# A hybrid decoder step on one core: token-row sums as a chain of their own, a new order for the first stage, and a shorter series for the decay

## The chip, the cores and the metric

The kernel runs on one core of a Trainium2 chip. The metric is device time in microseconds for one launch. Before the change three runs took 2071.05, 2072.48 and 2072.96 us; the median is 2072.48. One further execution was taken with the hardware profiler; it took 2066.42 us.

The engines are called as in the profile: PE (matmuls), PEld (its weight loads), DVE, ACT, POOL, and SP, which here only issues DMAs. An `ACTq` or `SPq` row is the issue of a DMA from that engine's queue.

## The reference

One layer of a hybrid decoder over 2048 prompt tokens and 8 decode tokens, width 1024:

```python
xn = _rmsnorm(x, norm1_g)
z = jnp.einsum('btd,de->bte', xn, w_in)
xr, gr, q, k, v = jnp.split(z, IN_SPLITS, axis=-1)
xc, new_conv = _causal_conv(xr, conv_buf, conv_w, conv_b)
hs, h_last = _rglru(xc, h0, ...)          # log_a = -8 * r * softplus(-lru_lambda)
rec = hs * jax.nn.gelu(gr)
att = _prompt_attention(q, k, v, sinks)   # sliding window 128, 8 heads, 2 kv heads, learned sinks
mix = concatenate([_rmsnorm(rec, rec_norm_g), _rmsnorm(att, attn_norm_g)])
h = x + jnp.einsum('bte,ed->btd', mix, w_out)
hn = _rmsnorm(h, norm2_g)
ff = jax.nn.silu(einsum(hn, w_gate)) * einsum(hn, w_up)
y = h + einsum(ff, w_down)                # then a final _rmsnorm; caches and states are returned too
```

The two places that the change edits in the computation are the mean of squares of each token's row, which `_rmsnorm(x, norm1_g)` needs, and `softplus(-lru_lambda)`, a value for each of the 512 channels of the recurrent branch. The rest of the change is order and time.

## The kernel before, in words

**Precision.** Every matmul is done as three: each operand is split into a rounded high part and the low rest, and `mm3` (matmuls at L388) adds high·high, high·low and low·high. A split of an activation costs one ACT pass (high, L417) and one DVE pass (low, L418); a split of a weight tile is a CAST on ACT (L360) and a subtraction on POOL (L361). Split weights of the input and output projections are stored to DRAM when first made (L380, `split_w`) and loaded back for later sub-blocks (L372).

**Stages.** The 2056 tokens are cut into four sub-blocks s = 0..3 (520 tokens, then three times 512). For each: `prep` loads the input transposed (`xs`, 8 tiles of 128 channels by 512 tokens) and splits it (`xn`); 14 units of the input projection (`ip{s}_{u}`) follow; then convolution, gates (`g`, ACT tanh into `ra` and `ia`) and scan for the recurrent branch; eight attention items per sub-block, each with scores `s`, exponentials into `sc`, transposes `pt` (copied to `pth` on ACT and `ptl` on DVE) and outputs `o` into `ratt`; two group norms (their sums are `st_rc`, `st_at`, their factors spread over partitions are `bc_rc`, `bc_at`); and the output projection `op`. After about 720 us only the feed-forward part (`ps_g`, `ps_u`, `pd`, `pw`) runs, in three token groups.

**Norm of the input.** The factor 1/rms of a token is not applied to `xn` but later, when the unit's PSUM is evicted: DVE multiplies by `rb_x`, the factors spread over all partitions (L743; outputs `xr`, `qraw`, `kraw`, `vraw`, `rrec`). For sub-block 0 the squares are summed over the transposed tiles. For sub-blocks 1 to 3 the tokens are also loaded as rows: `xt`, eight tiles of 128 tokens by 512 channels, 256 KB each, loaded by SP (L720) and squared on ACT with a running sum (L721). In `prep` one `xt` follows each `xs`; both take their buffers from the same pool `xsp`, which has two. After the eighth, `norm_rows` makes the factors: `xcols`, then `bc_x`, then `rb_x`.

**The decay's prologue.** `prologue` (from L607) computes softplus on DVE in tiles `sp` of 128 by 4 numbers with a series of ten terms: 1 + 8 x 2 + 1 instructions from L626 to L630. The convolution's gates of sub-block 0 need its result, `c` and `nc`.

**What sets the order.** Each of these functions is a generator that yields times. `Chains` runs them as events in order of these times, with keys such as ("xn", s) that one chain fires and another waits for. The time is the priority of the instructions, and a scheduler orders ACT, DVE, POOL and SP by it; `ahead(n)` gives an instruction a priority n earlier. The order of PE's matmuls is written out: `PE_ORDER` lists them by name with counts. Names with `w_` in front are fillers, matmuls on a matrix of ones whose result is overwritten. They go to the PSUM tile that the next matmul of that name uses. All engines and the DMA queues then run strictly in their own order, so an instruction that waits holds what stands behind it.

Of the kernel before, what the change touches and what calls it, by code (L numbers as in the profile page):

```python
# [13 lines left out]
P = 128  # L14
# [33 lines left out]
T_IP = [19.773, 89.475, 240.018, 361.589]  # L48
T_OP = [187.418, 329.004, 451.638, 498.253]
T_OPA, L_LM = 515.753, 37.593  # L50
# [75 lines left out]
ip1_0_0:6 dS:6 ip1_0_0:5 o3_0_0 ip1_0_0:4 ip1_12_0:2 dS2:2 ip1_12_0:2 pt3_0_1 o3_0_0 ip1_12_0:2 pt3_0_1:3
ip1_12_0:18 ip1_13_0:6 o3_0_1 ip1_13_0:2 o3_0_1 ip1_13_0:3 pt3_1_0:4 ip1_13_0:9 dS3 ip1_13_0 dS3 ip1_13_0:3
ip1_1_0:8 pt3_1_1:2 o3_1_0 pt3_1_1 ip1_1_0:2 pt3_1_1 o3_1_0 dS4:4 s4_0_0 ip1_1_0:2 dS4:4 o3_1_1 s4_0_1:4 s4_0_0:3
ip1_1_0 o3_1_1 ip1_1_0:11 ip1_5_0:6 dS5:2 s4_1_0:2 s4_1_1:4 ip1_5_0 vt1_1 ip1_5_0:3 s4_1_0:2 ip1_5_0:8 pt4_0_0:2
ip1_5_0 pt4_0_0:2 ip1_5_0:5 ip1_2_0:2 s5_0_0:4 ip1_2_0 s5_0_1:4 ip1_2_0 vt1_2 ip1_2_0:8 o4_0_0 ip1_2_0:6 pt4_0_1  # L130
o4_0_0 pt4_0_1:3 ip1_2_0:3 vt1_3 ip1_2_0:3 o4_0_1 s5_1_0:4 s5_1_1:4 o4_0_1 st_rc0 pt4_1_0:4 st_rc0:4 ip1_6_0:24
pt4_1_1:4 bc_rc0_0:3 s6_0_0:4 bc_rc0_0 s6_0_1:4 pt5_0_0 bc_rc0_4 pt5_0_0:3 g1_0_0_0 g1_0_1_0 w_st_at0:11 st_at0:5
ip1_3_0:24 ip1_7_0:8 bc_at0_0:4 ip1_7_0:16 op0_0_0:2 bc_at0_4 op0_0_0:10 op0_0_260:12 op0_1_0 g1_1_0_0 op0_1_0:11
op0_0_0 op0_0_260 op0_1_0 op0_0_260:2 op0_0_0:3 op0_1_0:6 op0_0_0:6 op0_1_0:3 op0_0_260:9 g1_1_1_0 op0_0_0:2
op0_1_0:2 o4_1_0:2 op0_1_260:4 o4_1_1:2 op0_1_260:20 op0_2_0:11 pt5_0_1:4 o5_0_0:2 op0_2_0:13 op0_2_260:13 s6_1_0:3
s6_1_1:4 s6_1_0 o5_0_1 op0_2_260:11 op0_3_0 g1_2_0_0 pt5_1_0 op0_3_0:12 o5_0_1 op0_3_0:2 pt5_1_0:3 op0_3_0:9
op0_3_260:17 g1_2_1_0 op0_3_260:7 op0_4_0:21 pt5_1_1:4 op0_4_0:3 op0_4_260:2 o5_1_0:2 op0_4_260:19 s7_0_0:4
op0_4_260:3 op0_5_0 o5_1_1 op0_5_0:12 pt6_0_0:4 op0_5_0 o5_1_1 op0_5_0:5 s7_0_1:4 op0_5_0:5 op0_5_260:7 g1_3_0_0
op0_5_260:17 o6_0_0 op0_6_0:3 pt6_0_1 o6_0_0 pt6_0_1:3 op0_6_0:5 g1_3_1_0 op0_6_0:10 o6_0_1 op0_6_0:6 op0_6_260
s7_1_0:4 s7_1_1:2 op0_6_260 s7_1_1:2 o6_0_1 op0_6_260 pt6_1_0:4 op0_6_260:21 op0_7_0:17 o6_1_0 bc_x2_0:3 pt6_1_1  # L140
o6_1_0 bc_x2_0 op0_7_0 pt6_1_1:3 op0_7_0:6 op0_7_260:5 o6_1_1 op0_7_260:19 ip2_4_0:24 o6_1_1 ip2_0_0:5 pt7_0_0:4
ip2_0_0:10 st_h0:5 ip2_0_0:2 o7_0_0 ip2_0_0:2 o7_0_0 ip2_0_0:5 ip2_5_0:4 pt7_0_1 st_rc1:2 pt7_0_1:3 st_rc1:2
ip2_5_0:9 pt7_1_0:4 ip2_5_0:2 o7_0_1 ip2_5_0:3 o7_0_1 bc_rc1_0:4 ip2_5_0:3 o7_1_0 ip2_5_0:3 pt7_1_1:3 ip2_1_0:2
pt7_1_1 ip2_1_0:8 g2_0_0_0 ip2_1_0:8 o7_1_0 ip2_1_0:4 o7_1_1 ip2_1_0:2 o7_1_1 g2_0_1_0 ip2_8_0:24 ip2_12_0:18
g2_1_0_0 ip2_12_0:6 ip2_9_0:23 g2_1_1_0 ip2_9_0 ip2_10_0:24 ip2_11_0:18 vt2_0 ip2_11_0:6 ip2_2_0:7 vt2_1 ip2_2_0:17
ip2_13_0:6 vt2_2 ip2_13_0:18 ip2_7_0:7 vt2_3 ip2_7_0:17 ip2_3_0:5 s8_0_0:4 s8_0_1:4 ip2_3_0:2 w_o8_0:2 st_at1:4
ip2_3_0:17 ip2_6_0 s8_1_0:4 s8_1_1 bc_at1_0:4 s8_1_1 pt8_0_0:3 s8_1_1 pt8_0_0 s8_1_1 ip2_6_0:7 s9_0_0:4 ip2_6_0:10
g2_2_0_0 ip2_6_0 o8_0_0 s9_0_1:4 ip2_6_0:5 op1_0_0:5 pt8_0_1 op1_0_0:2 o8_0_0 pt8_0_1:3 op1_0_0:4 g2_2_1_0
# [1556 lines left out]
```

## Time and profile before

| what | value |
|---|---|
| median of three runs | 2072.48 us |
| profiled execution | 2066.42 us, of which the span is 2064.6 us |
| PE busy | 2022.5 us, 98% |
| DVE, ACT, POOL busy | 1457.8, 945.4, 907.1 us |
| PE busy in 0 to 720 us | 693.80 us |
| PE busy in 720 to 2064 us | 1328.72 us |
| DMA | 450.98 MB, mean 218 GB/s |

The span is the time from the first to the last instruction in the trace. A row of the timeline tells start, length, engine, line, operation, output and inputs, and in brackets for how long the engine idled before and whose end released it. A row of a table by stage gives, for each engine, busy time and number of instructions, then the granted clock of PE (1.00 is full), the busy share of the 16 DMA engines and GB/s. Busy times of PE are modelled, since matmuls are pipelined. In a row like `L628 DVE TENSOR_TENSOR sp<-sp x8` the three numbers are the shortest, median and longest duration in ns, and the two times the first and last start.

### The profile page before, as it was taken

What the parts mean: (1) busy time and instruction counts of PE and PEld (TensorE: products, weight loads), DVE (VectorE), ACT (ScalarE), POOL (GpSimd) and SP (SyncE); (2) the same over time, 40 slices, a digit from 0 to 9 for tenths busy, and PEclk for the clock granted to TensorE, in tenths of its full rate; (3) what the DMA queues carried; (4) which work ended last, traced back from release to release, by engine and by line L of the source; (5) the groups of instructions that cost most, each with busy time, mean ns of one, the idle gap of its engine ahead of it and who ended that gap; (6) DMA issues with size and microseconds to landing.
All of it is one profiled execution on the core that took longest, in us unless ns stands there. A gap on an engine that the chain in (4) does not pass through costs nothing.

```text
span 2064.6 us, 34880 instructions
## 1 busy us (share of the span) xinstructions
PE 2022.5 (98%) x12328; PEld 1911.9 (93%) x12328; DVE 1457.8 (71%) x2702; ACT 945.4 (46%) x1960; POOL 907.1 (44%) x799
## 2 busy tenths in 40 slices
PE   8999899999999999999999999999999999999998
PEld 8988787878777899999999999999999999999998
DVE  7787785776996756666755667767767666777675
ACT  5764684563564543343334533334335433433343
POOL 5211343020122687657665655556556522322333
PEclk9999999999999999999999999999999999999999
DMA  8854485576687955655555777667677675566652
GB/s 302 272 203 149 153 299 168 183 258 195 205 267 261 329 201 203 219 209 207 199 190 191 251 255 245 232 228 229 211 255 265 215 246 193 187 195 195 197 179 96
DMA packets 208991, 450.98 MB, mean 218 GB/s; under 512 B 25232, under 2 KB 82720, under 8 KB 208800
## 3 DMA queue, kind: packets, MB, share of 16 engines
q1 hardware_dynamic: 205184, 445.73, 64.1%
q10 hardware_dynamic: 3632, 3.02, 0.4%
q8 instruction: 97, 1.59, 0.3%
q14 instruction: 78, 0.64, 0.1%
HBM read 335.89 MB, written 113.84 MB: 218 GB/s over the span
## 4 chain that ended last, share of the span: by engine, by line
PE 73%; DVE 11%; DMA 7%; ACT 4%; issue 3%; POOL 1%; SPq 0%; DVEq 0%; ACTq 0%; POOLq 0%
PE ps_u L388 18%; PE ps_g L388 18%; PE pd L388 11%; PE ip L388 10%; PE pw L388 9%; PE op L388 3%; DMA n<-hs 3%; DMA xt<-in_xR 1%; DMA mixed<-n 1%; PE o L388 1%; PE pt L393 1%; DVE sc L953 1%; PE s L388 1%; ACT sc L949 1%; DVE n L507 1%
## 5 line engine op out<-in xcount | busy, mean ns | idle before, releaser
L388 PE MATMUL ps_g<-hn,w_g 128*128 128x342 f32 (+1 forms) x2772 | 490.1, 320 | 3.2 <-DVE c_u L1386 1.8
L388 PE MATMUL ps_u<-hn,w_u 128*128 128x342 f32 (+1 forms) x2772 | 479.7, 319 | 0.5 <-ACT c_u L1412 0.4
L388 PEld LDWEIGHTS ps_g<-hn,w_g 128*128 128x128 f32 x2772 | 445.1, 188 | 5.2 <-DVE c_u L1386 2.7
L388 PEld LDWEIGHTS ps_u<-hn,w_u 128*128 128x128 f32 x2772 | 444.1, 188 | 1.1 <-ACT c_u L1412 0.7
L388 PE MATMUL ip<-xn,w_in 128*128 128x512 f32 (+1 forms) x1680 | 354.2, 358 | 4.5 <-DVE xr L743 2.0
L388 PEld LDWEIGHTS ip<-xn,w_in 128*128 128x128 f32 x1680 | 270.6, 189 | 50.4 <-issue 3.8
L1476 DVE TENSOR_TENSOR y<-y,pw 128x342 f32<-128x342 f32 x504 | 239.0, 504 | 75.1 <-PE pw L388 74.4
L388 PE MATMUL pd<-fh,w_d 128*128 128x344 f32 (+1 forms) x960 | 239.8, 320 | 0.0
L388 PE MATMUL op<-mix,w_out 128*128 128x512 f32 (+1 forms) x960 | 205.8, 360 | 0.1
L388 PEld LDWEIGHTS op<-mix,w_out 128*128 128x128 f32 x960 | 157.8, 192 | 28.7 <-issue 4.8
L1445 DVE TENSOR_TENSOR y<-y,pd 128x344 f32<-128x344 f32 (+1 forms) x240 | 117.9, 507 | 76.3 <-PE pd L388 71.5
L388 PEld LDWEIGHTS pd<-fh,w_d 128*128 128x128 f32 x960 | 168.3, 188 | 0.9 <-DVE y L1445 0.6
L388 PE MATMUL pw<-fh,wd 128*128 128x342 f32 x576 | 165.7, 320 | 2.1 <-DVE y L1476 2.1
L388 PE MATMUL pd<-fl,w_d 128*128 128x344 f32 (+1 forms) x480 | 153.5, 320 | 0.0
L1357 DVE TENSOR_TENSOR fl<-c_u,fh 128x342 fp32r<-128x342 f32 (+1 forms) x132 | 107.2, 817 | 45.5 <-ACT fh L1356 45.2
L1201 POOL TENSOR_TENSOR w_u<-ru,w_u 128x512 fp32r<-128x512 f32 x44 | 59.2, 1345 | 181.4 <-ACT w_u L1200 137.6
L1356 ACT CAST fh<-c_u 128x342 fp32r<-128x342 f32 (+1 forms) x132 | 63.1, 480 | 156.8 <-POOL c_u L1368 61.2
L1368 POOL TENSOR_TENSOR c_u<-c_u,c_g 128x342 f32<-128x342 f32 (+1 forms) x60 | 60.2, 1004 | 169.4 <-DVE c_u L1386 131.8
L388 PE MATMUL pw<-t,wd 128*128 128x342 f32 x648 | 126.8, 320 | 1.8 <-DVE t L1357 1.6
L1386 DVE TENSOR_TENSOR c_u<-c_u,ps_u 128x342 f32<-128x342 f32 (+1 forms) x99 | 50.3, 509 | 100.8 <-PE ps_u L388 100.5
L388 PEld LDWEIGHTS pw<-t,wd 128*128 128x128 f32 x648 | 106.0, 188 | 3.8 <-DVE t L1357 2.6
L388 PEld LDWEIGHTS pw<-fh,wd 128*128 128x128 f32 x576 | 105.3, 189 | 2.8 <-DVE y L1476 2.7
(313 smaller groups left out, 3509.7 us busy)
## 6 DMA issues: line engine op xcount, KB each, us to landing
w_g<-split_g SPq DMA_DIRECT2D x88, 512.0 KB, 4.2
w_u<-split_u SPq DMA_DIRECT2D x88, 512.0 KB, 4.6
w_in<-split_w SPq DMA_DIRECT2D x84, 512.0 KB, 3.6
rg<-in_wgate SPq DMA_DIRECT2D x110, 256.0 KB, 3.0
ru<-in_wup SPq DMA_DIRECT2D x110, 256.0 KB, 3.1
w_out<-split_w SPq DMA_DIRECT2D x48, 512.0 KB, 4.8
split_g<-w_g SPq DMA_DIRECT2D x44, 512.0 KB, 3.1
split_u<-w_u SPq DMA_DIRECT2D x44, 512.0 KB, 2.9
```

Of the source, the lines that this page charges most:

```text
L388: r = nc.tensor.matmul(*args, **kw)
L393: r = nc.tensor.transpose(*args)
L507: nc.vector.scalar_tensor_tensor(x, x, col(V_G2 + k), bc[n][:, :nn], ALU.mult, ALU.mult)
L949: nc.scalar.activation(sc[:, g, :kn + 1], sc[:, g, :kn + 1], AF.Exp, bias=mx[:, 0, g:g + 1], scale=-1.0, accum_out=mx[:, 1, g:g + 1])
L953: nc.vector.tensor_scalar(sc[:, g, :kn], sc[:, g, :kn], mx[:, 1, g:g + 1], None, ALU.mult)
L1201: lo_eng.tensor_tensor(w[:, 1, :], src, w[:, 0, :].bitcast(F32), op=ALU.subtract)
L1356: nc.scalar.copy(hi, v)
L1357: nc.vector.tensor_tensor(lo, v, hi.bitcast(F32), ALU.subtract)
L1368: (nc.vector if p == NPAIR - 1 or src is not v else eng(E_MUL[2 * h + n])).tensor_tensor(v, src, g, op=ALU.mult)
L1386: nc.vector.tensor_tensor(o, a, b, op)
L1445: r = nc.vector.tensor_tensor(ys[gi, n, m], ys[gi, n, m], ps, ALU.add)
L1476: nc.vector.tensor_tensor(v, v, ps, ALU.add)
```

## The change

Three things change. The series loses eight instructions: each multiply-and-add pair becomes one instruction, and the polynomial stays the same. The loads and squares of the token rows leave `prep` and become a chain `row_sums` with times of its own; `prep` waits for its key before `norm_rows`, and the sums get two buffers in turn. And the times, leads and `PE_ORDER` up to the first units of the feed-forward part are new.

```diff
-                v.tensor_scalar(t, s2, 1.0 / 19.0, 1.0 / 17.0, ALU.mult, ALU.add)
-                for n in (15, 13, 11, 9, 7, 5, 3, 1):
-                    v.tensor_tensor(t, t, s2, ALU.mult)
-                    v.tensor_scalar(t, t, 1.0 / n, None, ALU.add)
-                v.tensor_tensor(t, t, s, ALU.mult)
+                v.tensor_scalar(t, s2, 1.0 / 19.0, None, ALU.mult)
+                for n in (17, 15, 13, 11, 9, 7, 5, 3):
+                    v.scalar_tensor_tensor(t, t, 1.0 / n, s2, ALU.add, ALU.mult)
+                v.scalar_tensor_tensor(t, t, 1.0, s, ALU.add, ALU.mult)
...
                     xn.append(xt)
-                    if k == 0:
-                        sums = ap1.tile([P, 2, 4], F32, tag="xsums", name=f"xsums{s}")
+                fire(("xn", s))
+                yield t0 + dt * KD, ("sums", s)
+                norm_rows(s, None, state[s].pop("sums"))
+
+            def row_sums(s):
+                c0, _, _, w, _ = SUBS[s]
+                sums = ap1.tile([P, 2, 4], F32, tag=f"xsums{s % 2}", name=f"xsums{s}")
+                for k in range(KD):
+                    yield T_RS[s - 1] + D_RS[s - 1] * k
                     xt = xsp.tile([P, TM], F32, tag="xs", name=f"xt{s}_{k}")[:, :512]
                     j, h = k // 2, k % 2
-                    with ahead(10):
+                    with ahead(L_RS):
                         nc.sync.dma_start(xt, xR[c0 + j * w:c0 + (j + 1) * w, h * 512:h * 512 + 512])
                     nc.scalar.activation(xt, xt, AF.Square, scale=1.0 / 32, accum_out=sums[:, h, j:j + 1])
-                fire(("xn", s))
-                yield t0 + dt * KD
-                norm_rows(s, None, sums)
+                state[s]["sums"] = sums
+                fire(("sums", s))
...
                 ch.add(prep(s) if s else prep_first())
+                if s:
+                    ch.add(row_sums(s))
...
+T_RS, D_RS, L_RS = [70.767, 123.778, 299.952], [-6.135, 10.458, 8.043], 10.0
-T_RN = [127.174, 249.285, 358.664, 432.982]
+T_RN = [127.174, 248.552, 359.94, 444.16]
-T_ATT = [[-17.05, 7.329], [82.676, 5.648], [303.042, 13.458], [455.377, 9.304]]
-T_MIX0 = 394.361
+T_ATT = [[-8.444, 7.183], [88.337, 5.522], [305.073, 13.668], [455.377, 22.049]]
+T_MIX0 = 404.208
-bc_at3_0:4 op3_3_1:2 op3_2_1:12 op3_4_1:12 op3_6_1:12 op3_7_1:12 op3_5_1:12 g0_0_1:12 g0_0_2:11 w_ps_g0_0_5:7 g0_0_2
+g0_0_3:12 g0_0_4 w_ps_u0_0_2:4 g0_0_4:5 u0_0_2:9 g0_0_4 u0_0_2 u0_0_6:12 u0_0_2:2 g0_0_4:5 u0_0_5:12 u0_0_7:12
```

In `PE_ORDER` 72 fillers become 63: the seventeen of `st_x0` stay; of `bc_x1` one of five is left; `st_at0` has 13 instead of 11, `op3_0_0` 13 instead of 11; `g1_2_0_0` gets five, `bc_rc3` one, `pt15_0_0` and `o8_0` lose two and one; the sixteen of `ps_g0_0_5` go and `ps_u0_0_2` gets four. The matmuls of the computation are the same.

**ACT in the first stage**, around the copy of `rb_x` (the token factors of sub-block 0; `w_in_8` and `w_in_0` are weight tiles of units 8 and 0, `xc` is a convolution). Before:

```order
L360 CAST w_in_8_0_449<-raw_in_8_0_447 128x512
L360 CAST w_in_8_1_455<-raw_in_8_1_453 128x512
L456 COPY rb_x_305<-bc_x_0_306 128x416
L360 CAST w_in_0_0_513<-raw_in_0_0_511 128x512
L360 CAST w_in_0_1_519<-raw_in_0_1_517 128x512
L456 COPY rb_x_305<-bc_x_4_312 128x104
L761 ACTIVATE xc_1_436<-xr_1_315,vec 128x512
```

And after:

```order
L729 ACTIVATE xt_0_1422,xsums_155<-xt_0_1422 128x512
L729 ACTIVATE xt_1_1425,xsums_155<-xt_1_1425 128x512
L362 CAST w_in_8_0_444<-raw_in_8_0_442 128x512
L362 CAST w_in_8_1_450<-raw_in_8_1_448 128x512
L458 COPY rb_x_300<-bc_x_0_301 128x416
L362 CAST w_in_0_0_508<-raw_in_0_0_506 128x512
L458 COPY rb_x_300<-bc_x_4_307 128x104
L729 ACTIVATE xt_2_1428,xsums_155<-xt_2_1428 128x512
L768 ACTIVATE xc_1_431<-xr_1_310,vec 128x512
L778 DMA out_sconv_o<-xr_1_310 128x8
L729 ACTIVATE xt_3_1431,xsums_155<-xt_3_1431 128x512
L362 CAST w_in_0_1_514<-raw_in_0_1_512 128x512
```

The squares of sub-block 1's rows (`xt_0` to `xt_7`) now stand from before `w_in_8`'s casts to those of `w_in_10`; before, the first stood behind the cast of `w_in_4_0`, some forty rows later. On SP their loads stand in pairs between the raw loads of these weights. Sub-block 2's eight squares stand on ACT from behind the scan's `q_0` of sub-block 0 to the cast of `w_in_7_1` and just behind it, sub-block 3's first six where sub-block 2's stood.

**ACT at the first attention block of sub-block 1** (`pth_1_0`, `pth_1_1` and `sc_1` belong to its items, `w_out_0_0` is the first weight tile of the output projection). Before:

```order
L922 CAST qst_1_2512<-qraw 64x512
L963 CAST pth_1_0_2358<-pt_1_0_2353 128x512
L360 CAST w_out_0_0_3037<-raw_out_0_0_3035 128x512
L963 CAST pth_1_1_2367<-pt_1_1_2362 128x512
L949 ACTIVATE sc_1_2421,mx_1_2422<-sc_1_2421,mx_1_2422 128x257 x4
L456 COPY rb_rc_2223<-bc_rc_0_2224 128x416
```

And after:

```order
L929 CAST qst_1_2461<-qraw 64x512
L970 CAST pth_1_0_2354<-pt_1_0_2349 128x512
L970 CAST pth_1_1_2363<-pt_1_1_2358 128x512
L956 ACTIVATE sc_1_2417,mx_1_2418<-sc_1_2417,mx_1_2418 128x257 x4
L458 COPY rb_rc_2216<-bc_rc_0_2217 128x416
```

The cast of `w_out_0_0` has moved some fifteen rows down, behind `xc_1` of sub-block 1. In `PE_ORDER` the transposes `pt4_1_1`, which `pth_1_1` reads, now stand after fifteen instead of twenty-four matmuls of `ip1_6`.

**ACT some forty rows later, about where sub-block 0's output projection runs** (`xt_1` and `xn_2` belong to sub-block 2, `ia_1` and `pth_0_0` to sub-block 1). Before:

```order
L975 COPY ratt<-o_0_2891 64x4x128
L721 ACTIVATE xt_1_3580,xsums_3571<-xt_1_3580 128x512
L781 ACTIVATE ia_1_2830<-g_1_1_0_2834,hxb 128x512
L360 CAST w_out_3_0_3209<-raw_out_3_0_3207 128x512
L417 ACTIVATE xn_2_3585<-xs_2_3583,vec 128x512
L963 CAST pth_0_0_2405<-pt_0_0_2400 128x512
```

And after:

```order
L982 COPY ratt<-o_0_2895 64x4x128
L829 ACTIVATE gt_3_3045<-gt_3_3045 128x512
L419 ACTIVATE xn_2_3599<-xs_2_3597,vec 128x512
L419 ACTIVATE xn_3_3604<-xs_3_3602,vec 128x512
L788 ACTIVATE ia_1_2846<-g_1_1_0_2850,hxb 128x512
L362 CAST w_out_3_0_3227<-raw_out_3_0_3225 128x512
L970 CAST pth_0_0_2401<-pt_0_0_2396 128x512
```

The square `xt_1` is gone from here and `xn_2` and `xn_3` stand in front of `ia_1` and `pth_0_0`.

More of the change, by code (lines that the diff above doesn't have):

```diff
@@ L39 @@
 TP = 344
-U_IP, U_OP = 6.19, 5.41
+U_IP, U_OP = 6.191, 5.379
 N_EARLY = 3
-L_SS, L_ST = 9.0, 5.0
+L_SS, L_ST = 2.59, 5.729
 D_TB = 0.0
@@ L47 @@
 U_P = 2 * U_G + U_D
-T_IP = [19.773, 89.475, 240.018, 361.589]
-T_OP = [187.418, 329.004, 451.638, 498.253]
-T_OPA, L_LM = 515.753, 37.593
+T_IP = [19.526, 89.595, 239.473, 362.098]
+T_OP = [186.58, 329.023, 452.495, 496.569]
+T_OPA, L_LM = 515.753, 37.669
 T_B0 = 558.156
@@ L132 @@
[L132 to L136, printed above, removed]
@@ L184 @@
+u0_1_7:12 u0_1_4:12 u0_1_3:12
 """
```

153 lines of the change are left out of this document (79 added, 74 removed).

## The prediction

> **What bounds the kernel now.** I read the page first, then the busy time by stage, then TensorE's own waits in order of time, and last what stood in front of each wait. The page:
>
> ```profile
> span 2064.6 us, 34880 instructions
> PE 2022.5 (98%) x12328; PEld 1911.9 (93%) x12328; DVE 1457.8 (71%) x2702; ACT 945.4 (46%) x1960; POOL 907.1 (44%) x799
> ```
>
> TensorE (PE) is the bound; 42.1 us of the span are not PE time, and no edit removes a matmul of the computation. So the change can act on those 42 us, on the fillers and on the clock. By stage (length, then busy us of PE, PEld, DVE, ACT, POOL with instruction counts, granted clock, DMA share, GB/s):
>
> ```profile
> 0.00:80.00 80.00, 73.79 (x582) 71.85 (x583) 56.91 (x130) 43.23 (x91) 38.77 (x44) 1.00 0.86 298
> 80.00:131.00 51.00, 48.35 (x322) 43.03 (x320) 47.95 (x115) 43.75 (x99) 10.76 (x14) 1.00 0.71 236
> 200.00:240.00 40.00, 36.56 (x201) 29.75 (x200) 30.37 (x60) 23.84 (x51) 12.49 (x12) 0.96 0.38 132
> 240.00:300.00 60.00, 55.23 (x390) 50.96 (x389) 50.86 (x97) 48.22 (x98) 28.39 (x25) 0.94 0.80 270
> 720.00:2000.00 1280.00, 1273.27 (x8099) 1268.34 (x8098) 872.03 (x1483) 503.98 (x1030) 680.58 (x564) 1.00 0.64 217
> ```
>
> The long FFN stretch idles 6.7 us in 1280 and its order hardly changes: I give it nothing. The four earlier ones idle 6.2, 2.7, 3.4 and 4.8 us. PE's rows that begin after a wait, with two of fillers (start, busy, what, and in brackets the wait and who ended it):
>
> ```profile
> 33.07 0.74 PE L388 MATMUL ip<-xn,w_in 128*128 128x260 f32 x4 [2.03 <-DVE xr L743]
> 99.00 0.49 PE L388 MATMUL o<-pth,vt 128*128 128x512 f32 x1 [0.90 <-DVE ratt L976]
> 122.14 0.85 PE L388 MATMUL bc_x<-ones 128*128 128x256 f32 x5 [0.62 <-ACT ia L781]
> 130.95 0.51 PE L388 MATMUL o<-ptl,vt 128*128 128x512 f32 x1 [0.65 <-DVE ptl L964]
> 214.79 1.13 PE L388 MATMUL g<-xc,gw 128*128 128x512 f32 x2 [0.78 <-ACT ra L781]
> 217.65 1.58 PE L388 MATMUL st_at<-ones 128*128 128x256 f32 x11 [1.73 <-ACT ia L781]
> 252.77 0.66 PE L393 MATMUL pt<-cs,sc 128*128 128x128 f32 x4 [2.36 <-DVE ptl L964]
> 274.07 0.94 PE L393 MATMUL pt<-cs,sc 128*128 128x128 f32 x4 [2.02 <-DVE ptl L964]
> 446.96 0.50 PE L388 MATMUL o<-ptl,vt 128*128 128x512 f32 x1 [0.93 <-DVE ptl L964]
> 694.38 1.10 PE L388 MATMUL ps_g<-ones 128*128 128x256 f32 x7 [1.56 <-DVE xres L1113]
> 695.47 1.24 PE L388 MATMUL ps_g<-ones 128*128 128x256 f32 x9
> ```
>
> **The series (30 to 35 us).** The decay's prologue on DVE, the eviction behind it, and ACT:
>
> ```profile
> L628 DVE TENSOR_TENSOR sp<-sp x8: 161/161/1182, 26.8 to 30.6; 128x4 f32<-128x4 f32 x8
> L629 DVE TENSOR_SCALAR sp<-sp x8: 170/170/1153, 27.0 to 31.8; 128x4 f32<-128x4 f32 x8
> 32.59 0.42 DVE L743 TENSOR_TENSOR xr<-ip,rb_x 128x260 f32<-128x260 f32 x1
> 28.18 0.51 ACT L456 COPY rb_x<-bc_x 128x416 f32<-128x416 f32 x1 [4.49 <-PE bc_x L388]
> ```
>
> PE's wait at 33.07 ends with the eviction xr, which starts at 32.59 although its factor rb_x was there at 28.69: it queues behind the series. A step costs 0.2 us (starts 26.8 and 27.0), and one of each kind took 1.15 to 1.18. Eighteen steps become ten: 8 x 0.2 = 1.6 us less, and 2.0 more if the two slow ones are missed; so xr starts between 29.0 and 31.0 and the wait of 2.03 falls to between 0 and 0.4. What is late next are weight casts: on ACT two squares now stand before w_in_8's casts, and w_in_0_1's cast behind xt_2, xc_1 and xt_3. The 4.49 us in which ACT idles cover the first two if their loads have landed; for the other I allow 0.4. **Term -1.6** (ends -2.0 and +0.5).
>
> **Sub-block 1's rows (80 to 131 us).** All squares of this kernel, two ten-us windows, the load that PE's wait at 122.14 goes back to and its square, and two rows that date the new places:
>
> ```profile
> L721 ACT ACTIVATE xt<-xt x24: 612/630/635, 69.9 to 438.0; 128x512 f32<-128x512 f32 x24
>   DMA xt<-in_xR: 11.6, 8
> DMA to landing us min/median/max: 2.9/4.5/6.1
> 10.00:20.00 10.00, 9.62 (x79) 9.26 (x78) 9.90 (x12) 7.09 (x14) 4.79 (x3) 1.00 1.04 405
> 90.00:100.00 10.00, 9.10 (x60) 8.14 (x59) 9.84 (x21) 9.94 (x22) 2.80 (x3) 1.00 0.74 237
> 117.39 3.04 DMA xt<-in_xR
> 120.52 0.63 ACT L721 ACTIVATE xt<-xt 128x512 f32<-128x512 f32 x1 [1.32 <-DMA xt<-in_xR]
> 94.19 0.17 DVE L951 RECIPROCAL mx<-mx 128x4 f32<-128x4 f32 x1
> 97.43 0.63 ACT L822 ACTIVATE gt<-gt 128x520 f32<-128x520 f32 x1
> ```
>
> A square costs ACT 0.63 us plus 0.19 for the accumulator, and eight times ACT waited for its load, 11.6 us in all. Sub-block 1's eight squares leave a stretch where ACT is 99% busy; but sub-block 2's eight move in from later, at about 93 to 118 us. Up to 102 us the stretch loses one or two row operations (0.8 to 1.5 us) and may gain waits: xt_1's load can start only when the ring of two buffers is freed by DVE's xn_7, which now stands just before the reciprocal of 94.19; it lands 2.9 to 6.1 us later, and ACT's queue reaches its square right after the gt of 97.43: 0 to 3 us, and behind it stand ratt, pth and the table load for q. After 102 us the late xn and the 1.32 us wait are gone. I take the wait at 99.00 unchanged and most of 0.62 + 0.65 gone, less a little: **term -0.8** (ends -2.4 and +1.5). On SP the last four loads of sub-block 2 stand in a row, each waiting for the square two before it; a raw half of w_out, a store and w_in_10's reload queue behind them. PE uses w_in_10 only after bc_x1 (the row at 122.14) and the unit behind it, so I price this at nothing; with that cover gone it is part of the +1.5.
>
> The loads themselves go where DMA has less room (share 1.04 in 10 to 20 us). The Trainium skill's "DMA: Bandwidth & Descriptors", section "Issuing engines are not separate DMA queues", has all transfers share the same 16 engines and interleave, which speaks against putting rows beside the raw weights. It gives no price; mine stands with the rivals.
>
> **The stages 200 to 220 and 240 to 280 us.** ACT at both places, the load in front of the second, xn on DVE (one and two), and three windows:
>
> ```profile
> 208.42 0.62 ACT L360 CAST w_out<-raw_out 128x512 fp32r<-128x512 f32 x1 [5.68 <-PE ip L388]
> 248.28 0.63 ACT L721 ACTIVATE xt<-xt 128x512 f32<-128x512 f32 x1 [6.08 <-DMA xt<-in_xR]
> 243.64 4.55 DMA xt<-in_xR
> 250.88 1.24 DVE L418 SCALAR_TENSOR_TENSOR xn<-xs,vec,xn 128x512 fp32r<-128x512 f32 x1 [0.43 <-ACT xn L417]
> 250.00:260.00 10.00, 7.57 (x47) 6.90 (x45) 9.08 (x18) 9.95 (x24) 6.20 (x5) 0.83 0.82 271
> 270.00:280.00 10.00, 7.98 (x53) 7.62 (x52) 10.00 (x22) 9.32 (x23) 5.78 (x6) 0.83 0.90 287
> 30.00:40.00 10.00, 7.97 (x67) 7.76 (x66) 9.15 (x20) 3.96 (x7) 5.30 (x7) 1.00 0.71 245
> 241.32 2.44 DVE L418 SCALAR_TENSOR_TENSOR xn<-xs,vec,xn 128x512 fp32r<-128x512 f32 x2
> ```
>
> At 202.7 to 208.42 ACT's queue is blocked by one cast that needs a weight buffer which PE frees; the next pth and eight exponentials stand behind it. Moved behind xc_1, the cast frees them up to 5.7 us earlier, but PE now comes to pt4_1_1 nine matmuls sooner (about 2 us), and the gates after it still follow DVE and ACT one by one. Of 0.78 + 1.73 I take 1.2 off: **term -1.2** (ends -2.5 and +0.5).
>
> At 248.28 the square blocked pth_0_0 and so ptl, for which PE waited 2.36. Gone from there; in its place xn_2 and xn_3 wait for loads that start as DVE's xn_0 and xn_1 free the two buffers (242.5 and 243.7 by the last row; on SP's queue they pass a raw weight load): + 4.5 = 247.0 and 248.2 instead of 248.28, so pth comes 0 to 2 us earlier, about 1. The wait at 274.07 stands where DVE is full (10.00 of 10) and all eight xn now lie before it, at 0.7 to 1.2 us each, and six squares of sub-block 3 take the place of sub-block 2's seven on ACT: unchanged. **Term -1.0** (ends -3.0 and +1.0).
>
> **Clock.** Both windows with these waits were granted 0.83, a loss of 1.7 us in 10 and of 1.3 in PE's busy part; the 2.03 us wait at 33.07 brought none (1.00). A third lies in 200 to 240 (granted 0.96 over 40 us, 1.6 us). I count one of the three gone: **term -1.3** (ends 0 and -3.9). By the Trainium skill's "TensorE: Matmul & The Clock Gate", section "Why this matters for your kernels", only idle gaps above about 3 us throttle; the two rows at 0.83 disagree with it for waits of 2.0 to 2.4, the third agrees. By that page this term is zero and the sum -3.9.
>
> **The rest.** 446.96: two squares instead of seven remain near it, half of 0.93: -0.4. Fillers: the sixteen at 694.38 take 2.3 us by their rows (0.14 each) and hide nothing, since the wait before them had ended; they go, four stand elsewhere. But DVE and ACT behind them set the next waits, so I take -0.7 (ends -2.2 and 0). Elsewhere three more: +0.4 (ends 0 and +0.4). Newly set order: two new waits of the usual 0.7 us: +1.4 (ends 0 and +3).
>
> **Sum.** -1.6 - 0.8 - 1.2 - 1.0 - 1.3 - 0.4 - 0.7 + 0.4 + 1.4 = -5.2 us against the profiled execution (2066.42, of which the span is 2064.6): 2061.2. The median of the three runs is 2072.48, 6.1 above; on its scale 2067.3. A measurement of this kernel can tell about 0.2%, 4.1 us, from no change.
>
> **The rivals.**
>
> *The full engines keep their waits* (0.25). For it: DVE 10.00 of 10 and ACT 9.94 to 9.95 in the windows shown, refilled by sub-block 2's squares and the earlier xn. Against: ACT idled 5.68 and 6.08 us on its own queue there. Then only the series counts: -1.6 - 0.4 - 0.7 + 0.4 + 1.4 and a third of the 200 to 280 terms, -0.7: -1.6, 2070.9, within 0.2%.
>
> *Rows before weights* (0.12, slower). Eight loads of 256 KB stand ahead of raw weights on SP's queue at 12 to 45 us; at 405 GB/s each takes 0.65 us, 5.2 in all, and the casts behind an unlanded row wait too. For it: the DMA share of 1.04; against: 0.71 in 30 to 40. If the weights come later than PE by the whole of it, the series' gain (1.6) is lost, 5.2 added, and the same at xt_1 near 97 us costs 3.8: -5.2 + 10.6 = +5.4, 2077.9. It decides from where more than about 2 us of the 5.2 reach PE.
>
> *The clock returns* (0.15). Blocked queues were the whole cause: 1.73, 2.36 and 2.02 go, and the three slow windows: -5.2 - (6.1 - 2.2) - (3.9 - 1.3) = -11.7, 2060.8.
>
> *The clock does not answer* (0.08): the page's rule, or half-idle windows that remain: -3.9, 2068.6, just within 0.2%.
>
> That the rows' sums do not really come earlier is out: ACT's order shows sub-block 1's squares before its weights' casts of 30 us.
>
> **How the numbers follow.** The forecast has 0.40. Faster by over 0.2%: 0.40 + 0.15 = 0.55; within: 0.25 + 0.08 = 0.33; slower: 0.12. The range runs from the clock's return, 2060.8, past no change to 2074.5, which holds the lighter part of rows before weights; its full price, 2077.9, and what lies beside it are the 2 in 10 left out. The likeliest case alone, with its larger ends, spans 2063 to 2070.
>
> **What would show it.** Right: no PE wait above 0.5 us at 30 to 34; ACT without its 5.68 and 6.08 us waits; fewer windows at 0.83 before 300; no load of rows in the chain at 117; PE idle before 300 down from about 17 to 14 us. Wrong: waits of w_in's casts for raw loads at 30 to 60; ACT waiting for xt near 97; ptl still late at 250 and 273; or a difference that arises after 720.

## The result, and the profile after

| | before | after |
|---|---|---|
| median of the timed runs | 2072.96 us (5 runs, 2071.05 to 2075.74) | 2062.19 us (5 runs, 2058.85 to 2065.17) |
| profiled execution | 2066.42 us | 2061.57 us |
| its span, mean granted clock | 2064.6 us, 0.995 | 2059.8 us, 0.997 |

The ratio is 0.9945, with a 95% interval of 0.9926 to 0.9963; a second comparison, below, gave 0.9953 (0.9936 to 0.997). The change makes the kernel faster by about 0.5%, some 10 us, where 5.2 were forecast.

The two profiled executions differ by 4.8 us only, because the first one of before was among the fastest of that kernel: over the experiments below, 98 timed runs of before lie between 2064.28 and 2077.59 us with a mean of 2071.87, and 11 runs of after have a mean of 2062.73. So a stage of the profile pair shows where time went, and the timed runs show how much.

The page of after:

```profile
span 2059.8 us, 34860 instructions
PE 2018.7 (98%) x12319; PEld 1909.6 (93%) x12319; DVE 1463.0 (71%) x2694; ACT 944.2 (46%) x1960; POOL 905.3 (44%) x799
```

Of 4.8 us, PE's idle time gives 1.0 (42.1 to 41.1) and its busy time 3.8: nine fillers fewer, at 0.14 each 1.3; the rest, 2.5, goes with the higher granted clock (0.997 against 0.995), since the matmuls of the computation are the same. The stages of after (columns as in the prediction):

```profile
0.00:80.00 80.00, 76.52 (x585) 75.04 (x586) 56.66 (x131) 50.99 (x114) 39.99 (x45) 0.98 0.93 325
80.00:131.00 51.00, 49.46 (x330) 44.54 (x329) 46.51 (x111) 41.20 (x93) 11.31 (x14) 1.00 0.72 246
200.00:240.00 40.00, 36.18 (x210) 29.75 (x209) 34.80 (x57) 24.21 (x47) 12.47 (x11) 1.00 0.37 124
240.00:300.00 60.00, 56.06 (x412) 51.24 (x411) 53.25 (x98) 47.35 (x94) 27.79 (x26) 1.00 0.87 291
640.00:720.00 80.00, 75.00 (x407) 66.57 (x406) 54.35 (x73) 37.33 (x75) 44.32 (x31) 1.00 0.90 315
720.00:2000.00 1280.00, 1271.06 (x8081) 1265.62 (x8081) 875.52 (x1485) 502.53 (x1030) 672.86 (x563) 1.00 0.65 216
```

Read the second number against the first: PE idles 3.5 and 1.5 us in the first two stages where it idled 6.2 and 2.7; 3.8 instead of 3.4 in 200 to 240; 3.9 instead of 4.8 in 240 to 300, and both of these stages are now at full clock. But 640 to 720 idles 5.0 us where before idled 2.5, and the FFN behind it 8.9 instead of 6.7: part of what the first 300 us gain is given back after 640. PE's rows that begin after a wait, in order of time (some left out, among them 0.93 us at 693 and 1.01 at 700):

```profile
85.87 0.50 PE L390 MATMUL o<-pth,vt 128*128 128x512 f32 x1 [0.74 <-DVE ratt L983]
127.73 0.50 PE L390 MATMUL o<-ptl,vt 128*128 128x512 f32 x1 [0.36 <-DVE ptl L971]
209.88 1.12 PE L390 MATMUL g<-xc,gw 128*128 128x512 f32 x2 [0.78 <-ACT ra L788]
212.73 1.82 PE L390 MATMUL st_at<-ones 128*128 128x256 f32 x13 [1.73 <-ACT ia L788]
254.96 1.12 PE L390 MATMUL g<-xc,gw 128*128 128x512 f32 x2 [1.27 <-DVE xc L773]
268.41 0.63 PE L395 MATMUL pt<-cs,sc 128*128 128x128 f32 x4 [1.14 <-DVE ptl L971]
275.55 0.50 PE L390 MATMUL o<-ptl,vt 128*128 128x512 f32 x1 [0.97 <-DVE ptl L971]
685.36 4.04 PE L390 MATMUL ps_g<-hn,w_g 128*128 128x344 f32 x24 [1.18 <-DVE xres L1120]
698.41 0.40 PE L390 MATMUL ps_g<-hn,w_g 128*128 128x344 f32 x1 [1.32 <-DVE c_g L1395]
```

The 2.03 us at 33 are gone, and of the three waits between 99 and 131 only 0.36 is left. The pair at the gates near 210, 0.78 and 1.73, is there to the hundredth. The two waits of 2.36 and 2.02 for ptl have become two of 1.14 and 0.97, with a third of 1.27 for xc. At the start of the FFN PE ends the same wait for xres 9.0 us earlier than before (685.36 against 694.38) and loses 4.2 of that by the end.

### The profile page after: what moved, and what is told of

Its sections match the earlier page's. It is cut to its first block, busy times and chain, and to the rows that moved or that the text cites. A ratio compares the mean times of both kernels' runs of the same rounds, so it can differ in the third digit from the quotient of the medians.

```text
span 2059.8 us, 34860 instructions
## 1 busy us (share of the span) xinstructions
PE 2018.7 (98%) x12319; PEld 1909.6 (93%) x12319; DVE 1463.0 (71%) x2694; ACT 944.2 (46%) x1960; POOL 905.3 (44%) x799
## 4 chain that ended last, share of the span: by engine, by line
PE 73%; DVE 12%; DMA 7%; ACT 4%; issue 3%; POOL 2%; SPq 0%; DVEq 0%; ACTq 0%; POOLq 0%
PE ps_u L390 18%; PE ps_g L390 18%; PE pw L390 10%; PE ip L390 10%; PE pd L390 9%; PE op L390 3%; DMA n<-hs 3%; DMA mixed<-n 1%; DMA xs<-in_xT 1%; DVE sc L949 1%; PE o L390 1%; DVE n L509 1%; PE pt L395 1%; DVE xn L420 1%; DVE sc L960 1%
```

## The experiments

The theory from these two profiles was: sub-block 1's squares between its xn's held up the first 131 us, and the series only the wait at 33; the newly set order pays in the stages 200 to 300, through the clock and ptl; and the removed fillers pay nothing. The rivals were that the series or the order alone makes the difference, that the rows of sub-blocks 2 and 3 pay their part, and that only the runs' spread of clock is seen. Each run below was timed in five rounds against before on the same chip, whose median there is given as "beside". None leaves out work of the reference.

### Both kernels again

No edit. Before, unchanged:

> The kernel before, unchanged, a second profile of it. The first one took 2066.4 us, 6.1 under the median, so its span may miss waits that most executions have. Theory A (the profile was an unusually good draw): the ratio is 1.000 within 0.002, this profile takes 2069 to 2075 us, and PE's offsets against the first profile show where the extra 3 to 8 us arise (waits of the feed-forward part, or windows of 0.83 clock). Rival B (profiles are always shorter than the timed runs): 2066 to 2068 us again.

Measured 1.0005 (0.9994 to 1.0015), 2072.15 us beside 2071.5. Its profiled execution took 2071.53 us, 5.1 more than the first one of the same kernel. Three of its ten-us windows:

```profile
30.00:40.00 10.00, 7.97 (x54) 7.76 (x54) 7.69 (x20) 3.23 (x6) 4.13 (x6) 0.83 0.73 250
220.00:230.00 10.00, 9.23 (x51) 7.94 (x52) 9.83 (x16) 5.97 (x11) 3.08 (x3) 1.00 0.06 11
630.00:640.00 10.00, 7.81 (x42) 6.86 (x41) 4.96 (x12) 2.76 (x5) 2.26 (x2) 0.76 0.72 258
```

The last but two numbers are the granted clock. The first execution had 1.00 at 30 to 40 and 0.85 at 220 to 230; here it is the other way round. The window 30 to 40 has the same 7.97 us of PE work in both. Reduced clock follows a wait in some executions and not in others, so one profile's windows cannot be priced one by one.

After, unchanged:

> The changed kernel again, beside the three others of this job. Theory: ratio to before 0.995 within 0.001, mean granted clock about 0.996 where before has 0.9946, which is two half-speed windows (3.4 us) of the ten us. Rival (the first comparison was a lucky chip): 0.997 or more.

Measured 0.9953 (0.9936 to 0.997), 2062.33 us beside 2071.49. The result holds.

### The series alone

```diff
-v.tensor_scalar(t, s2, 1.0 / 19.0, 1.0 / 17.0, ALU.mult, ALU.add)
-for n in (15, 13, 11, 9, 7, 5, 3, 1):
-    v.tensor_tensor(t, t, s2, ALU.mult)
-    v.tensor_scalar(t, t, 1.0 / n, None, ALU.add)
-v.tensor_tensor(t, t, s, ALU.mult)
+v.tensor_scalar(t, s2, 1.0 / 19.0, None, ALU.mult)
+for n in (17, 15, 13, 11, 9, 7, 5, 3):
+    v.scalar_tensor_tensor(t, t, 1.0 / n, s2, ALU.add, ALU.mult)
+v.scalar_tensor_tensor(t, t, 1.0, s, ALU.add, ALU.mult)
```

> The kernel before with the shorter series alone; only DVE's prologue differs. Theory: PE's wait of 2.03 us at 33 falls to at most 0.4, PE is 1.6 to 2.0 us earlier at 41 us, and that lead lives on to the end: 1.6 us faster (ratio 0.999). Rival: ACT and DVE are full from 80 to 130 us and give the lead back there: PE 0 to 0.4 us earlier at 140 us, ratio 1.000.

Measured 0.9987 (0.9976 to 0.9997), 2068.31 us beside 2071.5. The first stage, its slice from 20 to 30, and then, in the timeline, the eviction behind the series:

```profile
0.00:80.00 80.00, 75.22 (x582) 73.39 (x583) 53.87 (x124) 44.30 (x95) 38.70 (x44) 0.98 0.87 300
20.00:30.00 10.00, 9.14 (x66) 9.15 (x67) 8.23 (x25) 2.12 (x5) 5.22 (x6) 0.83 0.82 285
```

```profile
30.17 0.43 DVE L742 TENSOR_TENSOR xr<-ip,rb_x 128x260 f32<-128x260 f32 x1 [1.23 <-ACT rb_x L456]
```

The wait at 33 is gone and the stage idles 4.8 us instead of 6.2; xr waits for its factor and no longer for DVE's queue. But this execution must be read with care: PE ran at 0.83 from 20 to 30, so everything that follows PE there came 1.5 us later, the factor too. A kernel with the short series at full clock is shown under the order below: there xr starts at 28.95, and no wait is left either.

The opposite edit, after with the long series put back (the same lines reversed):

> The changed kernel with the old series of eighteen steps; only DVE's prologue differs from the changed kernel. Theory: the wait at 33 returns with 1.6 to 2.0 us and stays to the end: ratio to before 0.9955 instead of 0.9945. Rival (the new order has room before 130 us): the loss is gone by 140 us, ratio 0.9945.

Measured 0.9955 (0.9943 to 0.9966), 2063.21 us, where after has 0.9945 and 0.9953. The wait that I had expected to return, 1.6 to 2.0 us, returned with 0.62. Inside the whole change the series is worth 0.4 to 2.1 us by these ratios and about 1 us by the medians, less than the runs can tell from nothing. The chain explains why.

### The chain alone, and its parts

Before with the chain of row sums, in the old order of PE and with the old series:

```diff
-                    if k == 0:
-                        sums = ap1.tile([P, 2, 4], F32, tag="xsums", name=f"xsums{s}")
+                fire(("xn", s))
+                yield t0 + dt * KD, ("sums", s)
+                norm_rows(s, None, state[s].pop("sums"))
+
+            def row_sums(s):
...
+                for k in range(KD):
+                    yield T_RS[s - 1] + D_RS[s - 1] * k
...
+                if s:
+                    ch.add(row_sums(s))
```

> The kernel before with the row sums as a chain of their own at the changed kernel's times, everything else (PE's order, all other times, the series) as before. Theory (blocked queues): the load at 117 and the 6.08 us wait of ACT at 248 are gone, PE's waits at 122, 131 and 252 fall from 3.6 to under 1.5 us, and it is 2 to 4 us faster (ratio 0.998 to 0.999). Rival (the new order makes the gain; the chain alone moves work into places that are not made ready for it): 0 to 4 us slower, with ACT waiting for weights or rows in 30 to 60 or near 97 us.

Measured 0.9973 (0.9959 to 0.9986), 2066.29 us beside 2071.5: half of the result with one of three parts, and more than the 2 to 4 us expected, though the wait at 252, which was to fall, rose to 3.00. Then the chain for sub-block 1 alone (sub-blocks 2 and 3 keep their squares in prep), and, with (2, 3) in the first line, for 2 and 3 alone:

```diff
+CHAINED = (1,)
...
-                if s:
+                if s in CHAINED:
                     ch.add(row_sums(s))
```

> The kernel before with a chain of its own for sub-block 1's row sums alone; sub-blocks 2 and 3 keep theirs in the preparation. Theory (most of the chain's gain is made where sub-block 1's eight squares leave the full stretch of ACT at 80 to 131 us and PE's order there stays): 4 to 5 of the chain's 6 us, ratio 0.9975 to 0.998; PE's idle time falls by 2 us before 80 and by 1 to 1.5 at 80 to 131. Rival (the blocked queue at 248 us is the larger part): 0.999 to 1.000.

> The complement: the kernel before with chains for the row sums of sub-blocks 2 and 3 alone. Theory: 0 to 2 us faster (0.999 to 1.000), since the 6.08 us wait of ACT at 248 goes but sub-block 2's eight squares fill the stretch before 118, which sub-block 1's have not left. Rival: 4 to 6 us faster (0.997 to 0.998).

Measured 0.9976 (0.9965 to 0.9987), 2066.77 us, for sub-block 1 alone, and 1.0006 (0.9993 to 1.0018), 2071.88 us, for 2 and 3: sub-block 1's eight squares are all of the chain's gain, as far as the intervals tell. The stages are read from the whole chain, whose profiled execution had full clock up to 131 us:

```profile
0.00:80.00 80.00, 76.21 (x586) 74.35 (x587) 58.57 (x139) 51.19 (x114) 39.82 (x45) 1.00 0.92 325
80.00:131.00 51.00, 49.85 (x338) 45.49 (x337) 47.45 (x112) 41.90 (x94) 10.55 (x14) 1.00 0.73 245
...
240.00:300.00 60.00, 51.89 (x374) 47.54 (x373) 50.39 (x93) 46.26 (x93) 25.41 (x24) 0.97 0.83 278
```

PE idles 3.8 and 1.2 us where before idled 6.2 and 2.7, together 3.9 less; sub-block 1's ratio says 5.0 (0.0024 of 2071.5). In 240 to 300 it idles 8.1 instead of 4.8; the largest part of this is that the second wait for ptl, 2.02 us in before, is 3.52 here. It is 3.44 to 3.52 in the three kernels of the old order that chain the rows of sub-blocks 2 and 3, and 1.98 to 2.25 in the four profiled executions of the old order that don't and have no extra fillers. So in the old order chaining these rows costs over 1 us here; by which instructions was not followed up. The prediction took this wait as unchanged.

That the first stage gains 2.4 with the long series still in place needs a reason. Here are ACT's casts after rb_x, POOL's splits that they release, and two steps of the series, in before:

```profile
28.58 1.14 ACT L360 CAST w_in<-raw_in 128x512 fp32r<-128x512 f32 x2
29.28 2.52 POOL L361 TENSOR_TENSOR w_in<-raw_in,w_in 128x512 fp32r<-128x512 f32 x2 [2.69 <-ACT w_in L360]
29.45 1.15 DVE L629 TENSOR_SCALAR sp<-sp 128x4 f32<-128x4 f32 x1
30.63 1.18 DVE L628 TENSOR_TENSOR sp<-sp 128x4 f32<-128x4 f32 x1
```

And the same place with the chain, with the eviction and PE's wait:

```profile
29.11 0.62 ACT L361 CAST w_in<-raw_in 128x512 fp32r<-128x512 f32 x1
33.16 0.24 ACT L457 COPY rb_x<-bc_x 128x104 f32<-128x104 f32 x1 [3.42 <-PE bc_x L389]
29.81 1.28 POOL L362 TENSOR_TENSOR w_in<-raw_in,w_in 128x512 fp32r<-128x512 f32 x1 [2.70 <-ACT w_in L361]
29.98 1.14 DVE L630 TENSOR_SCALAR sp<-sp 128x4 f32<-128x4 f32 x1
31.70 0.42 DVE L750 TENSOR_TENSOR xr<-ip,rb_x 128x260 f32<-128x260 f32 x1
32.17 0.75 PE L389 MATMUL ip<-xn,w_in 128*128 128x260 f32 x4 [0.60 <-DVE xr L750]
```

A step of 128x4 elements takes 0.16 to 0.17 us, but 1.14 to 1.18 while POOL splits a weight of 128x512. In before two casts release two splits, and two steps of the series are caught. With the chain the second cast has gone behind the other part of rb_x's copy, which waits for PE until 33.16, and behind squares; so POOL does one split, one step is caught, and PE waits 0.60 us instead of 2.03. Of this 1.43 the step not caught is 1.0; the other 0.4 comes from the pair of splits before, at 24 us, which caught DVE one step ahead of the series in before (L625, 3.43 us long) and only at its second step here (L629, 3.00). Chain and series remove the same wait, so their gains don't add: the chain leaves 0.6 us to the series, and the kernel above with the long series inside the whole change has nearly the same, 0.62 us at 31.75. The chain of sub-blocks 2 and 3, whose squares stand elsewhere, left this wait at 2.04.

### The order

Before with the chain and the series, in the old order (both diffs above):

> The kernel before with the chain and the short series, but the old order and times of everything else. What is missing to the changed kernel (0.995) is then the new order. Theory (the chain already takes most of the series' wait: 0.60 us are left of 2.03): little more than the chain alone, ratio 0.9965 to 0.997, and the new order gives the other 3 to 4 us. Rival (the parts add up): 0.9955, and the new order gives nothing on time.

And after with the rows put back into prep, so the new order and the series without the chain (the chain's diff reversed):

> The changed kernel with the row loads and squares put back into the preparation of the transposed tiles; all times, PE's order and the short series stay as changed. Theory (the chain is the larger part, the new order was set for it): most of the gain goes, ratio 0.998 to 1.001, with ACT waiting for row loads again near 117 to 120 and 248. Rival (the order makes the gain): 0.995 to 0.997.

Measured 0.9971 (0.9959 to 0.9984), 2065.39 us, and 0.9987 (0.9977 to 0.9997), 2070.36 us. All four with the short series:

| | rows in prep | rows as a chain |
|---|---|---|
| old order | 0.9987 | 0.9971 |
| new order | 0.9987 | 0.9945 and 0.9953 |

The new order gives nothing without the chain and some 4 to 5 us with it (0.0018 to 0.0026 of 2071). Where it pays is seen in the old order with chain and series, by two stages and by PE's waits in the second:

```profile
200.00:240.00 40.00, 36.57 (x177) 29.59 (x175) 27.38 (x50) 21.23 (x43) 11.93 (x11) 0.87 0.32 112
240.00:300.00 60.00, 52.13 (x376) 47.82 (x375) 51.83 (x95) 45.70 (x94) 26.63 (x23) 0.97 0.80 267
```

```profile
253.20 0.66 PE L394 MATMUL pt<-cs,sc 128*128 128x128 f32 x4 [2.77 <-DVE ptl L970]
275.92 1.04 PE L394 MATMUL pt<-cs,sc 128*128 128x128 f32 x4 [3.52 <-DVE ptl L970]
```

Here PE waits 2.77 and 3.52 us for the same two ptl; the stage idles 7.9 us, and 200 to 240 runs at 0.87. PE did not come earlier in this execution (its row of 245.02 in before starts at 245.04), so the longer waits are not a lead that is lost again. After idles 3.9 there, at full clock. Three profiled executions of the old order with the chain of sub-block 1 average 7.6 us idle in 240 to 300 and a clock loss of 4.7 us in 200 to 240 (the stage's length times what its granted clock lacks to 1); five of the new order with it average 3.9 and 0.6. And why the new order gives nothing with rows in prep, by two of PE's waits and their stage in that kernel:

```profile
112.83 0.50 PE L390 MATMUL ip<-xn,w_in 128*128 128x512 f32 x1 [3.36 <-ACT xn L419]
114.50 1.65 PE L390 MATMUL ip<-xn,w_in 128*128 128x512 f32 x3 [1.17 <-DVE xn L420]
```

```profile
80.00:131.00 51.00, 43.44 (x274) 38.56 (x272) 41.93 (x98) 39.69 (x88) 10.35 (x12) 0.93 0.64 201
```

In the new order PE comes to sub-block 1's xn before they are ready when the squares stand between them, and the stage idles 7.6 us instead of 1.5. Order and chain belong together. What in the new order does it stays open: the order of PE's matmuls, the fillers and the times of the other engines changed together, and no run separates them. In this kernel, at full clock up to 80 us, the short series alone had removed the wait at 33:

```profile
28.95 0.42 DVE L744 TENSOR_TENSOR xr<-ip,rb_x 128x260 f32<-128x260 f32 x1
```

The last experiment on the chain was in the new order, after with the rows of sub-blocks 2 and 3 back in prep:

```diff
+CHAINED = (1,)
...
-                if s:
+                if s in CHAINED:
                     ch.add(row_sums(s))
```

> The changed kernel with the row sums of sub-blocks 2 and 3 put back into the preparation; sub-block 1 keeps its chain, and the new order and the short series stay. Theory (the new order's 3 to 5 us are made at 200 to 300 us because sub-block 2's rows have left that stretch): they go, ratio 0.9965 to 0.9975, ACT waits for a row load again near 245 and more windows of 0.83 come back there. Rival (only sub-block 1's chain matters, in this order too): 0.995.

Measured 0.9945 (0.9931 to 0.9959), 2061.99 us beside 2074.03. I had expected the new order to need those rows, and that fell. Its stage 240 to 300:

```profile
240.00:300.00 60.00, 56.80 (x415) 52.10 (x415) 52.44 (x103) 50.15 (x98) 30.81 (x27) 1.00 0.89 305
```

PE is busy 56.8 us here and 56.1 in after. The squares that the prediction saw blocking ACT in this stage cost PE nothing when they stand there in the new order; what counts is that order as a whole.

### The fillers

After with the sixteen fillers restored where before has them, and the four new ones taken away:

```diff
-g0_0_2:12 g0_0_5:12
+g0_0_2:11 w_ps_g0_0_5:7 g0_0_2 w_ps_g0_0_5:9 g0_0_5:12
...
-g0_0_4 w_ps_u0_0_2:4 g0_0_4:5
+g0_0_4:6
```

> The changed kernel with the sixteen fillers at the start of the feed-forward part put back and the four new ones left out. Theory (DVE and ACT set the next waits there): no difference, ratio within 0.0005 of the changed kernel, PE's waits between 685 and 705 shrink by about what the fillers take (2 us). Rival (the fillers cost what their rows say): 1.5 to 2 us slower than the changed kernel.

Measured 0.9944 (0.993 to 0.9958), 2060.84 us beside 2071.49, so the same as after. PE's waits and fillers there, and the stage:

```profile
685.56 1.10 PE L391 MATMUL ps_g<-ones 128*128 128x256 f32 x7 [1.36 <-DVE xres L1121]
686.66 1.23 PE L391 MATMUL ps_g<-ones 128*128 128x256 f32 x9
694.23 4.04 PE L391 MATMUL ps_g<-hn,w_g 128*128 128x344 f32 x24 [0.66 <-ACT c_g L1422]
698.98 1.21 PE L391 MATMUL ps_g<-hn,w_g 128*128 128x344 f32 x6 [0.71 <-DVE c_g L1396]
```

```profile
640.00:720.00 80.00, 77.27 (x427) 69.27 (x426) 53.08 (x72) 37.84 (x76) 45.23 (x32) 1.00 0.90 318
```

With the sixteen, 2.3 us by their rows, the stage idles 2.7 us, without them 5.0: the removed fillers turned into waits of about their length. DVE and ACT end these waits.

### The clock held up by fillers

Before with eleven more fillers ahead of st_at0 (near 217 us) and twelve ahead of pt5_1_1 (near 274 us), to see whether work in the waits brings the clock back, and time with it:

```diff
-g1_0_0_0 g1_0_1_0 w_st_at0:11 st_at0:5
+g1_0_0_0 g1_0_1_0 w_ip1_3_0:11 w_st_at0:11 st_at0:5
...
-op0_4_0:21 pt5_1_1:4
+op0_4_0:21 w_op0_4_260:12 pt5_1_1:4
```

> The kernel before with eleven and twelve more fillers that run inside two of PE's waits (before st_at0 near 217 us, into a bank that is free, and before pt5_1_1 near 274 us); a few of ACT's and DVE's instructions near 274 move by some rows. No work of the computation moves earlier. Theory (a half-idle stretch of about 3.4 us brings a half-speed window): the windows after these waits are granted 1.00, the mean clock rises by 0.001 to 0.0016 and the kernel is 2 to 3.4 us faster (ratio 0.9985). Rival (only gaps above 3 us throttle, the drops come from elsewhere): clock and time unchanged, ratio 1.000, or up to 1.001 where fillers run over the end of the wait.

Measured 1.0017 (1.0007 to 1.0027), 2075.31 us beside 2071.49: slower.

```profile
219.25 1.58 PE L388 MATMUL ip<-ones 128*128 128x256 f32 x11 [2.51 <-DVE rrec L743]
273.41 1.66 PE L388 MATMUL op<-ones 128*128 128x256 f32 x12
275.57 0.63 PE L393 MATMUL pt<-cs,sc 128*128 128x128 f32 x4 [0.50 <-DVE ptl L964]
```

Against what I had expected, the first group's PSUM bank was not free: the group waited itself, 2.51 us until DVE had evicted the bank, and then stood in front of PE's work for 1.6. The second did run inside the wait (2.02 became 0.50), and the window was granted 1.00. The mean clock rose by 0.0004, at most 0.9 us if the whole span follows it, and the kernel lost 3.5 us; the first group alone took 0.8 more waiting and 1.6 of PE's time. As a test of clock against time it is inconclusive.

## Why the prediction was right, point by point

The direction was right and the size half. That the time fell inside the range is in part luck: two terms failed (200 to 220 and the fillers, 1.9 of the 5.2 us), one came out for another reason than the stated one (240 to 280), and sub-block 1's rows, priced at a sixth of what they gave, made up for them. Term by term:

**The series, -1.6.** The mechanism is shown: the wait is gone with the short series alone, which is worth 2.7 us (0.13%). Within the whole it is worth about 1 us, for a reason that the step missed: it noted that w_in_0_1's cast goes behind squares and allowed 0.4 us for its being late. It didn't ask whom that cast had disturbed, which is the series, through POOL's split.

**Sub-block 1's rows, -0.8.** This is the mis-sized term. That chain alone is worth 5.0 us. The idle time of the first two stages fell by 3.9 with the chain, of which 1.4 are the wait at 33; 1.5 lie in 80 to 131, twice what the step gave, and 1.0 in smaller waits before 80. Of this 1.0, 0.7 lies before 20 us, where the second execution of before also idles less than the first (2.5 against 3.3 us), and so need not be the chain's. The whole is firm: the eight profiled executions with this chain idle 2.6 to 3.8 us in the first 80, the six without it 4.7 to 6.4. The cost that the step set against it was small: ACT's wait for xt near 97 came out at 1.09 us of a possible 3, as this row of after shows, and PE's wait at 99 was not unchanged but gone, with 0.74 at 85.87 in its place.

```profile
101.63 0.63 ACT L729 ACTIVATE xt<-xt 128x512 f32<-128x512 f32 x1 [1.09 <-DMA xt<-in_xR]
```

And the sum of ACT's waits for row loads (us in all, times):

```profile
  DMA xt<-in_xR: 3.7, 3
```

ACT waited 3 times for a row load, 3.7 us in all, instead of 8 times and 11.6.

**200 to 220, -1.2.** This step failed. The cast left ACT's queue as foreseen, and the gates' waits stayed at 0.78 and 1.73. The cast that reads pt4_1_1 in after:

```profile
203.58 0.58 ACT L970 CAST pth<-pt 128x512 fp32r<-128x512 f32 x1 [4.03 <-PE pt L395]
```

ACT has been free for 4.03 us and waits for PE: its blocked queue was not what these gates hung on. The 0.78 is ACT's row ra, which starts as PE's matmuls of the gate end, and the 1.73 is ACT's way from ra to ia without a pause, over casts of mix and the activation a: it starts ra at 214.05 and ia at 216.91 in before, 209.13 and 211.99 in after, 2.86 us apart in both. The change left these rows as they were. What the stage gained is clock (0.96 to 1.00), and the repeats (1.00 for before, 0.96 for after) show that as chance.

**240 to 280, -1.0.** Measured -0.8 in the stage (4.8 to 3.9 idle), so the size is right. Its cause is not: the squares in ACT's queue cost nothing there when put back, and the old order with the chain idles 7.9. The new order as a whole makes the difference, and that the size came out is luck.

**Clock, -1.3.** Larger: the mean granted clock of the timed runs rose from 0.9944 to 0.9958, which over 2064 us is 2.9 us, an estimate that lets the whole span follow the clock. Over the 98 runs of before the time falls by only 1.3 us for each 0.001 of clock, which would make it 1.8. The mechanism assumed, a window per wait, is too simple. In after these two windows alone were reduced before 700 us:

```profile
20.00:30.00 10.00, 9.16 (x67) 9.12 (x67) 7.86 (x26) 3.33 (x9) 5.23 (x6) 0.83 0.97 344
620.00:630.00 10.00, 8.07 (x47) 6.97 (x47) 5.69 (x10) 5.08 (x10) 2.26 (x2) 0.83 0.77 275
```

The three that before lost between 220 and 280 are gone, though waits of 1.73 and 1.27 remain, and there is a new one at 20 to 30, where PE idles 0.84 us. It appeared in the profiled executions of some of these kernels and not of others: the same stretch had full clock in after with the sixteen fillers (where 0 to 10 was reduced instead), and in after with sub-blocks 2 and 3 in prep. The rule of the Trainium skill's "TensorE: Matmul & The Clock Gate", section "Why this matters for your kernels", that idle gaps above about 3 us throttle, would, read as a limit, have put this term at zero: the rows disagree with it on both sides of the change. They don't give another rule.

**446.96, -0.4.** The stages 300 to 540 together gained 0.7 (idle 1.4 to 0.7) in this pair, and 0.3 between the second executions (2.3 to 2.0). About right, as far as this scatter tells.

**Fillers, -0.7, and +0.4 elsewhere.** The first failed: the sixteen hid the waits behind them, and taking them away gained nothing. The step had named this end (0) and chosen the middle.

**New waits, +1.4.** The profile pair shows 4.7 us more idle time after 640 (2.5 in 640 to 720, 2.2 behind), of which 2.3 replace fillers; the others are 2.4.

The sum of 5.2 came out too small because the first 131 us were priced at 2.4 (series and rows), where the kernel with chain and series in the old order gained 6.0 in all (0.0029 of 2071.5; 3.9 of it are idle time in its first 131 us), and the clock below what it gave by either estimate. Of the 9.1 us between the means of the timed runs, 1.8 to 2.9 are clock; the profiled executions (two of before, five of the new order with the chain) show 2.3 of idle time and nine fillers 1.3. The other 2.6 to 3.7 lie in no stage that the traces agree on; traced executions are few beside runs that spread over 13 us, and this stays open.

**The rivals.** "The full engines keep their waits" holds for 200 to 220 and not for 240 to 280. "Rows before weights" didn't happen: between 12 and 131 us two splits of POOL (0.72 us at 55 and 0.28 at 60) and one cast of ACT (0.37 at 56) wait for a raw load, less than in before (a split of 3.70, casts of 0.92 and 1.65), though the DMA share of the first stage rose from 0.86 to 0.93. "The clock returns" came near in time (11.7 forecast, about 10 measured) but not in its reason, since the waits at 200 to 280 remained. "The clock does not answer" is not borne out: the mean clock rose. Of the signs named, no wait above 0.5 at 30 to 34, ACT's queue freed, no load of rows in the chain at 117, and fewer windows of reduced clock came as said; PE's idle time before 300 fell from 17 to 13. The signs against came weakly: a cast's wait of 0.37 for a raw load, ACT's 1.09 for xt, the 1.14 and 0.97 left for ptl, and a difference after 720, a loss.

## What to carry to other kernels

When work moves on one engine, ask also what it now holds back and whom that had disturbed: here a cast that went behind squares on ACT put off one of POOL's splits, and this freed DVE. An edit that pays in one place can cost in another: the row sums of sub-blocks 2 and 3 added over 1 us to a wait in the old order and cost nothing in the new. Two edits that remove the same wait don't add, and an order set for one arrangement of loads may be worth nothing with another, so they are to be timed in all four combinations. Fillers in front of a stage that another engine paces cost nothing, and removing them buys nothing; and one profile is not enough where executions of one kernel spread by 0.6%.

## What the runs showed of the hardware

Small DVE instructions stretch by one micro-second and more beside POOL's tensor work: 128x4 steps of 0.16 to 0.17 us took 1.14 to 1.18, and in after one step of the short series, beside two splits that POOL began at 24.00, took 3.0:

```profile
24.00 2.52 POOL L363 TENSOR_TENSOR w_in<-raw_in,w_in 128x512 fp32r<-128x512 f32 x2
```

```profile
L630 DVE SCALAR_TENSOR_TENSOR sp<-sp x8: 161/164/2998, 23.5 to 27.8; 128x4 f32<-128x4 f32 x8
```

The second is from the view of one tile, with the shortest, median and longest step in ns: one of eight is 18 times the median, and it started at 23.54 and so ended as POOL did (26.54 and 26.52). Not all that DVE does is stretched: with the series alone, two evictions of 128x260 from PSUM at 32.53 and 32.88 took their usual 0.43 and 0.42 us beside a pair of splits that ran from 30.74 to 33.28. The length of a series of tiny steps matters less than whether it meets such a split.

Reduced clock of one ten-us window, about 0.83, came at different places in executions of one unchanged kernel (30 to 40 or 220 to 230). In the two executions each of before and after, the windows of 0.83 to 0.85 hold or follow PE waits between 0.84 and 2.4 us, and the same waits stood at full clock in other executions.
